# Layer 2's recurrence: half of the state scalings and most of the corner-block copies move from VectorE to ScalarE

## The chip, the cores and the metric

The program runs on one NeuronCore of a Trainium2 chip, in one launch. The metric is the device time in microseconds (us). The core's engines are named in the profile's short forms: PE (TensorE, matmuls), PEld (its weight loads), DVE (VectorE), ACT (ScalarE), POOL (GpSimd) and SP (SyncE, which issues most DMAs). Each engine runs its own instructions in program order and waits for the others on semaphores.

## The reference, cut to what matters

The model is one step of a decoder of four layers with a different token mixer in each. The prompt has 16 learned rows and 256 tokens, and eight sample sequences of 8 tokens ride along, so that 336 rows are carried through every layer. Layer 2 is RWKV-7 time mixing: 32 heads of 64 by 64 state, with a decay, and a rank-one correction of the state, at each token.

```
    def step(s, inp):
        r_t, w_t, k_t, v_t, a_t, b_t = inp
        sa = jnp.einsum('bhvk,bhk->bhv', s, a_t)
        s = s * w_t[:, :, None, :] + sa[..., None] * b_t[:, :, None, :] + v_t[..., None] * k_t[:, :, None, :]
        return s, jnp.einsum('bhvk,bhk->bhv', s, r_t)

    s_new, y = lax.scan(step, s0.astype(F32), (tm(r), tm(decay), tm(k), tm(v), tm(-kk), tm(kk * a)))
    ...
    out = (yn + bonus).reshape(b, l, D_INNER).astype(xn.dtype) * g
    return (xn[:, -1].astype(x_prev.dtype), s_new.astype(s0.dtype)), out @ p['w_o']
```

## The kernel before, in words

`layer2` replaces the token-by-token loop by chunks. The 336 rows make six units of 64 rows (`NU` is 6; unit 0 holds the samples, units 1 to 5 the prompt). The 32 heads are worked in 16 pairs (`KE` is 16; index `p`), one head on partitions 0 to 63 and one on 64 to 127, which is why most operations of this stage come twice, each on 64 partitions. A chunk needs the inverse of a unit triangular matrix. Its two 32 by 32 diagonal blocks are inverted row by row on DVE (`invert`: the products `tmpi` and the sums into `LT`), for all pairs in four lanes; the last lane still runs during the first six pairs of the recurrence.

Four functions, written as generators, make up the stage that the change touches:

- `before(p)` prepares a pair. It projects the values (`pvv`, 24 matmuls), builds the off-diagonal corner of the inverses in two products on PE (`pAZ`), and copies the result of each out of PSUM, two copies of 32 by 192 each: into `A_` (the second product's operand) and then into the right half of the tile `s.Z` (`Zr` in the profile). Then come the samples' start states (`pX`, copied to `x`) and the values transposed (`pvt`, copied into `SV` by DVE).
- `recur(p)` goes through the six units one after the other. In a unit: a product into `pch` and its copy `xs` (ACT); from unit 2 on the scaling `sd` of the carried state by the chunk's decay, one instruction of 64 by 64 per head; the product of the inverse with `xs`, and its copy into `SV` (ACT), over the rows that `sd` has read; then the state product, and one DVE instruction per head that multiplies it by the decay and adds `sd` (written `SV`, or `wo` in the last unit), and the output product into `pY`.
- `after(p)` normalises a finished pair: `ch` and `cl` are the two halves of `pY`, then `pm`, `sq`, `rln` (1 / the standard deviation, on ACT), `y`, and the gate's product on POOL.
- `sample(p)` updates the samples' states (`sx`, `S` on POOL and DVE, `pD` on PE).

Pair `p` takes two rounds of 18 slots; in each round the second half of one pair (units 3, 4, 5) runs beside the first half of the next (units 0, 1, 2). So unit 5 of `p` and unit 2 of `p + 1` are side by side, and their four scalings follow each other. The order inside a round is fixed by the table `PLAN` ("before", "after", "weights", "sample", "lanes" give the slots), and the four compute engines keep exactly this order (`InOrder`). In the rounds a weight block is split into high and low halves as well: `whi` on ACT, `wlo` on POOL.

The PSUM tile `pch` of a pair also holds the input of `rln`, so the next state product of the other half of that tile stands behind the read by `rln`. The start product of the next-but-one pair writes `pY` and stands behind the copy `cl<-pY` on DVE.

Of the kernel before, what the change touches and what calls it, by code (L numbers as in the profile page):

```python
# [12 lines left out]
AF = mybir.ActivationFunctionType  # L13
# [9 lines left out]
NS = 8  # L23
# [28 lines left out]
HB = 32  # L52
# [182 lines left out]
MUL, ADD, SUB = ALU.mult, ALU.add, ALU.subtract  # L235
# [193 lines left out]
def blocks(t):  # L429
    return [t[:, j] for j in range(t.shape[1])]  # L430
# [11 lines left out]
def dense_steps(k, out, parts, xh, xl, k0=0, n=8):  # L442

    hi, lo = parts
    for j in range(n):
        kk = k0 + j
        first, last = kk == 0, kk == len(xh) - 1
        k.nc.tensor.matmul(out, lo[:, j, :], xh[kk], start=first, stop=False)  # L448
        k.nc.tensor.matmul(out, hi[:, j, :], xl[kk], start=False, stop=False)  # L449
        k.nc.tensor.matmul(out, hi[:, j, :], xh[kk], start=False, stop=last)  # L450
        yield
# [902 lines left out]
def layer2(k, O):  # L1354
    nc, tc, A = k.nc, k.tc, k.A
# [10 lines left out]
    WC = keep.tile([P, KE, NS + NU - 1], F32, name="WC")  # L1366
# [296 lines left out]
    for n in range(2 * KE + 2):  # L1663
        p, t0 = n // 2, 8 * n
# [103 lines left out]
    top, low = ([slice(hp * HD + o, hp * HD + o + HB) for hp in range(2)] for o in (0, HB))  # L1768

    def before(p, x=None):  # L1770

        s = st[p]
        if p:
            pvv = k.ps.tile([P, 512], F32, tag="mm", name="pvv")[:, :N]
            x = dense_steps(k, pvv, W[p], blocks(vh), blocks(vl))
        else:
            x = iter(())
        ab = Ab[p % 2]
        for hp in range(2):
            nc.gpsimd.tensor_copy(ab[ss[hp], :, hp], s.A0[ss[hp]].rearrange("p w (b t) -> p b w t", t=TS))  # L1780
        for _ in range(3):
            next(x, None)
            yield

        pAZ = k.ps.tile([P, 512], F32, tag="az", name="pAZ")
        n = NU * HB
        A_ = tw.tile([P, NU, HB], F32, tag="A_", name="A_", bufs=1)
        for u in range(NU):
            for hp in range(2):
                nc.tensor.matmul(pAZ[low[hp], u * HB : (u + 1) * HB], s.L[top[hp], u], s.Z[top[hp], u, HB:], start=True, stop=True)  # L1790
        yield
        for hp in range(2):
            nc.vector.tensor_copy(A_[low[hp]].rearrange("p u c -> p (u c)"), pAZ[low[hp], :n])
        yield
        for _ in range(2):
            next(x, None)
            yield
        for u in range(NU):
            for hp in range(2):
                nc.tensor.matmul(pAZ[top[hp], n + u * HB : n + (u + 1) * HB], A_[low[hp], u], s.Z[low[hp], u, HB:], start=True, stop=True)  # L1800
        yield
        for hp in range(2):
            nc.vector.tensor_copy(s.Z[top[hp], :, HB:], pAZ[top[hp], n : 2 * n].rearrange("p (u c) -> p u c", c=HB))
        yield
        next(x, None)
        yield
        pX0 = k.ps.tile([P, 512], F32, tag="az", name="pX0")[:HD, : NS * 4 * TS]
        s.x0 = tw.tile([P, 2, NS, TS], F32, tag="x0", name="x0")
        for half in range(2):
            for b in range(half * NS // 2, (half + 1) * NS // 2):  # L1810
                nc.tensor.matmul(pX0[:, b * 4 * TS : (b + 1) * 4 * TS], s.S0[:, b], ab[:, b].rearrange("p g w t -> p (g w t)"), start=True, stop=True)
            if half == 0:
                for _ in range(2):
                    yield
                    next(x, None)
                if p:
                    nc.vector.tensor_copy(s.v[:, :N], pvv)
            yield
        pvt = k.ps.tile([P, 512], F32, tag="mm", name="pvt")[:, :NB]
        for j in range(3):  # L1820
            nc.tensor.transpose(pvt[:, j * P : (j + 1) * P], s.v[:, j * P : (j + 1) * P], k.ident)
        for hp in range(2):
            nc.scalar.copy(s.x0[vs[hp]].rearrange("p w b t -> p b w t"), pX0.rearrange("p (b g w t) -> p b g w t", g=2, w=2, t=TS)[:, :, hp])
        yield
        for j in range(2):
            for hp in range(2):
                nc.vector.tensor_copy(s.sv[vs[hp], j::2, hp], pvt[ss[j]].rearrange("p (u g c) -> p u g c", g=2, c=HD)[:, :, hp])
            yield
# [3 lines left out]
    def recur(p):  # L1832

        s = st[p]
        sv, G = s.sv, s.G
        s.c = k.ps.tile([P, 512], F32, tag=f"c{p % 2}", name="pch")
        pX, pA, pS = (s.c[:, j * HD : (j + 1) * HD] for j in (0, 0, 1))
        for u in range(NU):
            for hp in range(2):
                rows = slice(0, P) if u > 1 else vs[hp]  # L1840
                nc.tensor.matmul(pX[ss[hp]], G[rows, 0, hp, u], sv[rows, u, hp], start=True, stop=u > 0)
                if u == 0:
                    nc.tensor.matmul(pX[ss[hp]], s.x0[vs[hp], 1].rearrange("p b t -> p (b t)"), k.ident[vs[hp], vs[hp]], start=False, stop=True)
            xs = tw.tile([P, HD], F32, tag="xs", name="xs", bufs=2)
            nc.scalar.copy(xs, pX)
            yield
            if u == 0:
                s.Y = k.ps.tile([P, 512], F32, tag="Y", name="pY")[:, :NB]
            py = [s.Y[h, u * CH : (u + 1) * CH] for h in ss]
            if u > 1:  # L1850
                sd = tw.tile([P, HD], F32, tag="sd", name="sd", bufs=2)
                for hp, h in enumerate(ss):
                    nc.vector.tensor_scalar(sd[h], sv[h, u, hp], WC[h, p, NS + u - 1 : NS + u], None, op0=MUL)
            yield
            for hp in range(2):
                nc.tensor.matmul(pA[ss[hp]], s.Z[ss[hp], u], xs[ss[hp]], start=True, stop=True)
            yield
            for hp, h in enumerate(ss):
                if u > 1:
                    nc.tensor.matmul(py[hp], sv[h, u, hp], s.R[h, u], start=True, stop=False)  # L1860
                if u == 0:
                    nc.tensor.matmul(py[hp], k.ident[vs[hp], vs[hp]], s.x0[vs[hp], 0].rearrange("p b t -> p (b t)"), start=True, stop=False)
            for hp, h in enumerate(ss):
                nc.scalar.copy(sv[h, u, hp], pA[h])
            yield
            if u > 0:
                for hp in range(2):
                    nc.tensor.matmul(pS[ss[hp]], G[:, 2, hp, u], sv[:, u, hp], start=True, stop=True)
                if u < NU - 1:
                    o = [sv[h, u + 1, hp] for hp, h in enumerate(ss)]  # L1870
                else:
                    wo = tw.tile([P, HD], F32, tag="wo", name="wo", bufs=1)
                    o = [wo[h] for h in ss]
                for h, q in zip(ss, o):
                    d = WC[h, p, NS + u - 1 : NS + u]
                    if u == 1:
                        nc.vector.tensor_scalar(q, pS[h], d, None, op0=MUL)
                    else:
                        nc.vector.scalar_tensor_tensor(q, pS[h], d, sd[h], op0=MUL, op1=ADD)
            yield  # L1880
            for hp in range(2):
                nc.tensor.matmul(py[hp], sv[:, u, hp], G[:, 1, hp, u], start=u == 1, stop=True)
            if u == NU - 1:
                nc.sync.dma_start(O["wkv_p"][:, p], wo)
            yield
# [93 lines left out]
    def evacuate(i, out):  # L1979
        if items[i][0] is A["l2_v"]:  # L1980
            nc.scalar.copy(st[items[i][1]].v[:, :N], out)
            steps_.append(before(items[i][1]))
        else:
            gated(out)
# [49 lines left out]
    for t in range((KE + 1) * NT):  # L2034
        i, p = t % NT, t // NT - 1
# [30 lines left out]
        if i + 1 == NT and p + 3 < KE:  # L2066
            plan(before(p + 3), t, PLAN["before"])
# [333 lines left out]
```

## Time and profile before

| | |
|---|---|
| time before, median of 3 runs | 1878.07 us (1877.92 to 1886.85) |
| the profiled execution's own time | 1878.39 us |
| its span | 1876.5 us |
| mean granted TensorE clock | 0.953 of full speed |
| PE busy | 1738.5 us (93%) |
| DVE busy | 1213.3 us (65%) |
| ACT busy | 743.1 us (40%) |
| POOL busy | 641.4 us (34%) |
| first and last scaling `sd` | 1113.4 us and 1398.9 us |

Times inside the span count from the span's start. The rounds of the recurrence stand between about 1103 and 1402 us, some 300 us of the 1876.5. Line 382 is a helper that records almost every instruction of this stage, so instructions are told apart by their tiles. A row of the timeline gives the start, the time from the first to the last of the merged instructions, the engine, the operation, and in brackets how long the engine stood idle before and what ended that.

### The profile page before, as it was taken

The page shows a single profiled execution, that of the slowest core. Times are in us where ns is not written, and L with a number is a line of the kernel's source. Part 1 is how long each engine was busy: PE and PEld are TensorE (multiplying, and loading weights), DVE is VectorE, ACT ScalarE, POOL GpSimd, SP SyncE. Part 2 cuts the span into 40 slices and gives each one's busy share as a digit, 9 for nine tenths or more (in the row PEclk, how much of TensorE's full clock was granted, in tenths as well). Part 3 has the DMA queues.
Part 4 walks back from the last instruction along what each step waited for, and adds up shares of the span by engine and source line. Part 5 has one row for each costly group of instructions (what it writes and reads, how often), then busy time and mean ns, then how long its engine had stood idle before and what let it go on. Part 6 is the DMA issues. An engine that isn't in the chain of part 4 may idle for free. (4 is left out here: it accounts for less than half of the span.)

```text
span 1876.5 us, 32699 instructions
## 1 busy us (share of the span) xinstructions
PE 1738.5 (93%) x12302; PEld 1366.1 (73%) x12302; DVE 1213.3 (65%) x2304; ACT 743.1 (40%) x1738; POOL 641.4 (34%) x825
## 2 busy tenths in 40 slices
PE   4998897999999997999999998899989799999997
PEld 2666596867779996666666886677769578778776
DVE  8999547596435455655787858677765736355453
ACT  2553243432145343443445343355554324143332
POOL 5667334000000025434345343344446414142212
PEclk9999898999999998999998998789999899999998
DMA  5564544554564443356556864466623457666551
GB/s 194 136 169 130 129 150 142 162 170 132 152 169 151 142 147 99 115 173 194 176 180 190 246 199 133 126 192 187 183 90 102 149 179 242 216 198 240 180 192 68
DMA packets 199695, 306.16 MB, mean 163 GB/s; under 512 B 115601, under 2 KB 133777, under 8 KB 197041
## 3 DMA queue, kind: packets, MB, share of 16 engines
q1 hardware_dynamic: 178384, 265.84, 47.5%
q0 software_dynamic: 10592, 32.72, 5.3%
q10 hardware_dynamic: 10560, 5.51, 1.0%
q8 instruction: 97, 1.59, 0.4%
q14 instruction: 62, 0.50, 0.1%
HBM read 225.04 MB, written 78.97 MB: 162 GB/s over the span
## 5 line engine op out<-in xcount | busy, mean ns | idle before, releaser
L411 DVE TENSOR_TENSOR wlo<-wst,whi 128x1024 fp32r<-128x1024 f32 x138 | 171.2, 1242 | 158.1 <-ACT whi L407 132.2
L407 ACT CAST whi<-wst 128x1024 fp32r<-128x1024 f32 (+1 forms) x125 | 129.3, 1035 | 92.4 <-PE pr L450 39.1
L382 PE MATMUL pg<-x_n,wst 128*128 128x336 f32 x512 | 160.8, 458 | 0.0
L382 POOL TENSOR_TENSOR wlo<-wst,whi 128x512 fp32r<-128x512 f32 (+1 forms) x57 | 74.2, 1302 | 145.3 <-ACT whi L382 142.8
L382 PEld LDWEIGHTS pg<-x_n,wst 128*128 128x128 f32 x512 | 93.5, 191 | 41.4 <-issue 0.9
L382 PE MATMUL pu<-x_n,wst 128*128 128x336 f32 x352 | 114.8, 467 | 2.3 <-DVE x_n L491 1.8
L382 PE MATMUL pkr<-xr,wst 128*128 128x336 f32 x256 | 99.5, 485 | 0.0
L382 PEld LDWEIGHTS pu<-x_n,wst 128*128 128x128 f32 x352 | 67.7, 199 | 35.8 <-issue 3.2
L382 PEld LDWEIGHTS pgm<-AR,BK 64*128 64x128 f32 x384 | 58.2, 190 | 45.3 <-issue 25.2
L2311 DVE SCALAR_TENSOR_TENSOR s<-s,pn 128x512 f32<-128x512 f32 x64 | 43.8, 684 | 70.2 <-PE pn L2310 70.0
L569 POOL TENSOR_TENSOR sums<-sums 128x336 f32<-128x336 f32 x19 | 22.6, 1202 | 194.6 <-ACT sums L567 191.1
L382 ACT CAST whi<-wst 128x256 fp32r<-128x256 f32 (+1 forms) x117 | 68.0, 586 | 50.4 <-issue 14.1
L382 DVE TENSOR_TENSOR G<-pgm,gmask 128x128 f32<-128x128 f32 x192 | 46.3, 284 | 56.0 <-PE pgm L382 55.8
L382 PE MATMUL pgm<-AR,BK 64*128 64x128 f32 x384 | 80.2, 316 | 1.3 <-ACT G L382 1.3
L382 PE MATMUL pkr<-xk,wst 128*128 128x336 f32 x256 | 75.9, 446 | 0.0
L382 PEld LDWEIGHTS pch<-SV,Gr 128*64 128x64 f32 (+1 forms) x704 | 33.8, 145 | 56.6 <-ACT rln L382 20.0
L2312 POOL DMA_DIRECT2D out_ret_s<-s x32 | 17.2, 539 | 147.1 <-DVE s L2311 147.1
L450 PE MATMUL pz<-gh,whi 128*128 128x336 f32 x208 | 66.0, 317 | 0.0
L382 PEld LDWEIGHTS pkr<-xk,wst 128*128 128x128 f32 x256 | 48.7, 190 | 23.6
L448 PE MATMUL pz<-gh,wlo 128*128 128x336 f32 x208 | 65.9, 317 | 0.0
L449 PE MATMUL pz<-gl,whi 128*128 128x336 f32 x208 | 65.9, 317 | 0.0
L382 PE MATMUL pch<-SV,Gr 128*64 128x64 f32 (+1 forms) x704 | 51.0, 252 | 14.6 <-ACT rln L382 7.5
(807 smaller groups left out, 5374.6 us busy)
## 6 DMA issues: line engine op xcount, KB each, us to landing
wst<-in_l_in SPq DMA_DIRECT2D x64, 512.0 KB, 4.0
dG<-G SPq DMA_DIRECT2D x16, 1152.0 KB, 5.2
wst<-in_l_out SPq DMA_DIRECT2D x32, 512.0 KB, 3.8
wst<-in_l_glu SPq DMA_DIRECT2D x32, 512.0 KB, 3.8
wst<-in_l_g SPq DMA_DIRECT2D x32, 512.0 KB, 4.6
wst<-in_l_v SPq DMA_DIRECT2D x32, 512.0 KB, 4.6
s<-in_l_s SPq DMA_DIRECT2D x32, 512.0 KB, 4.1
out_ret_s<-s POOLq DMA_DIRECT2D x32, 512.0 KB, 4.8
```

What stands on the lines that cost most here:

```text
L382: return lambda *a, **kw: tc.keep_in_program_order(getattr(e, name)(*a, **kw))
L407: k.nc.scalar.copy(hf, st)
L411: e.tensor_tensor(lf[:, a:b], st[:, a:b], hf[:, a:b].bitcast(F32), op=ALU.subtract)
L448: k.nc.tensor.matmul(out, lo[:, j, :], xh[kk], start=first, stop=False)
L449: k.nc.tensor.matmul(out, hi[:, j, :], xl[kk], start=False, stop=False)
L450: k.nc.tensor.matmul(out, hi[:, j, :], xh[kk], start=False, stop=last)
L569: (nc.vector if m == KD - 1 and name != "xx" else nc.gpsimd).tensor_tensor(sums[name], sums[name], t, op=ADD)
L2311: nc.vector.scalar_tensor_tensor(s[:, d], s[:, d], math.exp(TS * LOG_G[h]), pn, op0=MUL, op1=ADD)
L2312: nc.gpsimd.dma_start(O["ret_s"][h, b], s)
```

## The change

In `before(p)` a name `copy` is ScalarE's copy for the first eight pairs and VectorE's for the others; the two copies into `A_` and the two into `Zr` go by it. In `recur(p)` the scalings `sd` of the even pairs become ScalarE activations with the function Copy and the decay as a scale operand per partition; those of the odd pairs stay on VectorE. No PE, POOL or DMA instruction changes its place, and no activation table is loaded that wasn't before.

```
+        copy = nc.scalar.copy if p < 8 else nc.vector.tensor_copy
...
-            nc.vector.tensor_copy(A_[low[hp]].rearrange("p u c -> p (u c)"), pAZ[low[hp], :n])
+            copy(A_[low[hp]].rearrange("p u c -> p (u c)"), pAZ[low[hp], :n])
...
-            nc.vector.tensor_copy(s.Z[top[hp], :, HB:], pAZ[top[hp], n : 2 * n].rearrange("p (u c) -> p u c", c=HB))
+            copy(s.Z[top[hp], :, HB:], pAZ[top[hp], n : 2 * n].rearrange("p (u c) -> p u c", c=HB))
...
-                    nc.vector.tensor_scalar(sd[h], sv[h, u, hp], WC[h, p, NS + u - 1 : NS + u], None, op0=MUL)
+                    d = WC[h, p, NS + u - 1 : NS + u]
+                    if p % 2:
+                        nc.vector.tensor_scalar(sd[h], sv[h, u, hp], d, None, op0=MUL)
+                    else:
+                        nc.scalar.activation(sd[h], sv[h, u, hp], AF.Copy, scale=d)
```

On DVE, early in the round in which pair 0 does units 3 to 5: two scalings and two copies stand between the inversion's steps (`tmpi`, `LT`).

```order
 L382 TENSOR_TENSOR tmpi<-LT 128x135
 L382 TENSOR_TENSOR LT<-LT,tmpi 128x27x5
-L382 TENSOR_SCALAR sd<-SV_8904,WC 64x64 x2
-L382 COPY A__9850<-pAZ 32x192 x2
 L382 TENSOR_TENSOR tmpi<-LT 128x156
 L382 TENSOR_TENSOR LT<-LT,tmpi 128x26x6
```

Both leave DVE there; the inversion's steps close up.

On DVE, at the end of the next round, where unit 5 of pair 1 (`SV_8905`) and unit 2 of pair 2 (`SV_8906`) are side by side, ahead of the copies of the transposed values and the last state of pair 1:

```order
 L382 TENSOR_TENSOR LT<-LT,tmpi 128x18x14
 L382 TENSOR_SCALAR sd<-SV_8905,WC 64x64 x2
-L382 TENSOR_SCALAR sd<-SV_8906,WC 64x64 x2
 L382 COPY SV_8904<-pvt 64x3x64 x4
 L382 SCALAR_TENSOR_TENSOR wo<-pch,WC,sd 64x64 x2
```

Two of the four scalings leave DVE; the odd pair's two stay.

On ACT, the same place, in the kernel before:

```order
L382 COPY xs<-pch 128x64 x2
L382 COPY x_10201<-pX_10200 64x8x2x8 x2
L382 CAST whi<-wst 128x256
L382 COPY SV_8905<-pch 64x64 x2
L382 COPY SV_8906<-pch 64x64 x2
L382 ACTIVATE rln<-pch,b_10257 128x336
```

and in the changed kernel:

```order
L382 COPY xs<-pch 128x64 x2
L382 ACTIVATE sd<-SV_8906,WC 64x64 x2
L382 COPY x_10201<-pX_10200 64x8x2x8 x2
L382 CAST whi<-wst 128x256
L382 COPY SV_8905<-pch 64x64 x2
L382 COPY SV_8906<-pch 64x64 x2
L382 ACTIVATE rln<-pch,b_10257 128x336
```

The two scalings of the even pair stand between `xs` and the copies into `SV`, one after the other, and `rln` follows.

## Rows read from the trace of the kernel before

**Rows 1.** Busy time by stretch: length, PE, PEld, DVE, ACT, POOL, clock, DMA.

```profile
1115.00:1133.00 18.00, 15.30 (x225) 11.77 (x225) 15.91 (x42) 6.33 (x26) 6.23 (x7) 1.00 0.35 90
1280.00:1300.00 20.00, 19.30 (x292) 14.88 (x291) 14.93 (x43) 11.36 (x40) 9.26 (x10) 1.00 0.70 201
```

**Rows 2.** DVE's timeline: the last states of pairs 0, 1, 5 and 6.

```profile
1132.47 0.60 DVE L382 SCALAR_TENSOR_TENSOR wo<-pch,WC,sd 64x64 f32<-64x64 f32 x2
...
1150.65 0.60 DVE L382 SCALAR_TENSOR_TENSOR wo<-pch,WC,sd 64x64 f32<-64x64 f32 x2
...
1241.36 0.60 DVE L382 SCALAR_TENSOR_TENSOR wo<-pch,WC,sd 64x64 f32<-64x64 f32 x2 [0.93 <-ACT rln L382]
...
1257.29 0.60 DVE L382 SCALAR_TENSOR_TENSOR wo<-pch,WC,sd 64x64 f32<-64x64 f32 x2 [0.93 <-ACT rln L382]
```

**Rows 3.** PE's timeline, 1115 to 1225 us: matmuls before which PE stood idle.

```profile
1115.32 0.34 PE L382 MATMUL pch<-SV,Gr 128*64 128x64 f32 x4 [0.41 <-ACT SV L382]
...
1119.78 0.34 PE L382 MATMUL pch<-SV,Gr 128*64 128x64 f32 x4 [0.46 <-ACT SV L382]
...
1122.29 0.60 PE L382 MATMUL pch<-SV,Gr 128*64 128x64 f32 x8 [1.06 <-DVE SV L382]
...
1131.40 0.34 PE L382 MATMUL pch<-SV,Gr 128*64 128x64 f32 x4 [0.68 <-ACT SV L382]
...
1133.75 0.60 PE L382 MATMUL pch<-SV,Gr 128*64 128x64 f32 x8 [0.66 <-DVE SV L382]
...
1139.78 0.60 PE L382 MATMUL pch<-SV,Gr 128*64 128x64 f32 x8 [0.70 <-DVE SV L382]
...
1150.15 0.45 PE L382 MATMUL pch<-SV,Gr 128*64 128x64 f32 x8 [1.56 <-ACT rln L382]
...
1155.99 0.33 PE L382 MATMUL pY<-x,ident 64*64 64x64 f32 x4 [2.18 <-DVE cl L382]
...
1172.77 0.45 PE L382 MATMUL pch<-SV,Gr 128*64 128x64 f32 x8 [1.00 <-ACT rln L382]
...
1196.30 0.45 PE L382 MATMUL pch<-SV,Gr 128*64 128x64 f32 x8 [0.74 <-ACT rln L382]
...
1219.41 0.45 PE L382 MATMUL pch<-SV,Gr 128*64 128x64 f32 x8 [0.37 <-ACT rln L382]
...
1224.80 0.33 PE L382 MATMUL pY<-x,ident 64*64 64x64 f32 x4 [1.79 <-DVE cl L382]
```

**Rows 4.** The scalings: all of them (ns min/median/max), then one place in the timeline.

```profile
L382 DVE TENSOR_SCALAR sd<-SV,WC x128: 233/253/1354, 1113.4 to 1398.9; 64x64 f32<-64x64 f32 x128
...
1147.07 2.18 DVE L382 TENSOR_SCALAR sd<-SV,WC 64x64 f32<-64x64 f32 x4
1147.08 1.27 POOL L382 TENSOR_TENSOR wlo<-wst,whi 128x512 fp32r<-128x512 f32 x1 [3.74 <-ACT whi L382]
...
1148.49 1.06 ACT L382 COPY SV<-pch 64x64 f32<-64x64 f32 x4 [1.48 <-DVE sd L382]
```

**Rows 5.** Groups by shape, 1103 to 1402 us: busy us, mean ns, idle before.

```profile
L382 ACT COPY xs<-pch 128x64 f32<-128x64 f32 x96 | 19.4, 212 | 81.3 <-PE pch L382 74.7 <-DVE tmpi L382 3.6 <-DVE SV L382 2.3
L382 ACT ACTIVATE rln<-pch,b 128x336 f32<-128x336 f32 x15 | 8.1, 540 | 0.2
L382 ACT COPY x<-pX 64x128 f32<-64x128 f32 x30 | 7.7, 258 | 2.8 <-PE pX L382 2.6
...
L382 DVE COPY Zr<-pAZ 32x192 f32<-32x192 f32 x30 | 10.5, 350 | 18.2 <-PE pAZ L382 17.9
```

**Rows 6.** ACT's timeline between `xs` and `SV`, where pair 4 does its unit 5.

```profile
1216.62 0.53 ACT L382 COPY x<-pX 64x128 f32<-64x128 f32 x2 [0.18 <-PE pX L382]
...
1217.95 0.86 ACT L382 COPY SV<-pch 64x64 f32<-64x64 f32 x4 [0.49 <-PE pY L382]
```

**Rows 7.** Two stretches around a fall of the clock, columns as in rows 1.

```profile
1222.20:1225.60 3.40, 1.61 (x44) 1.16 (x42) 2.93 (x7) 0.97 (x4) 2.42 (x4) 1.00 0.52 151
1225.60:1229.00 3.40, 3.40 (x28) 2.31 (x25) 3.13 (x9) 2.53 (x4) 1.04 (x1) 0.59 0.64 178
```

## The prediction

> **What bounds the kernel now.** The change touches only layer 2's rounds, so I read that stage alone. First the busy time by stretch [rows 1]. From 1280 to 1300 us, a stretch without the inversion, PE is busy 19.30 of 20 us: PE bounds it. From 1115 to 1133, with the inversion's steps on DVE, PE is busy 15.30 of 18 and DVE 15.91: there DVE sets the pace. ACT has 6.33 of 18 us in use and 11.36 of 20.
>
> Then the distance between the last states of successive pairs gives the time of a round [rows 2]: 1150.65 - 1132.47 = 18.18 us for pair 1's, (1241.36 - 1150.65) / 4 = 22.68 for those of pairs 2 to 5, and 1257.29 - 1241.36 = 15.93 for pair 6's. Against the last, which is PE's own pace, the rounds with the inversion lose 2 to 7 us each.
>
> Where these go, PE's own waits tell [rows 3]. The reader is to see three kinds. In the rounds of pairs 0 and 1, PE waits for copies into SV by ACT or for states by DVE. At a pair's end it waits for `rln`: 1.56, 1.00, 0.74, 0.37 us. And a little later it waits 2.18 and 1.79 for `cl` (the same wait, about 2 us, stands in the rounds of pairs 3 and 4 too). The last kind also moves the clock [rows 7]: in the 3.4 us to 1225.6 PE is busy 1.61 us at the full clock, and in the next 3.4 the granted clock averages 0.59, since it falls to its lower level (1.2 GHz). This happens once in each of the rounds of pairs 2 to 5 and makes 18.18 into 22.68, so one such fall costs about 4.5 us.
>
> **What the scalings do there** [rows 4]. Most of the 128 take 253 ns, the longest 1354. At 1147.07 four of them take 2.18 us, the first beside a POOL product that runs from 1147.08 to 1148.35. ACT's copies into SV overwrite what the scalings read; ACT has been idle 1.48 us for them, `rln` follows those copies, and PE's 1.56 us is the end of this chain. So a scaling can cost PE more than its own time.
>
> **Removed from DVE.** 64 scalings and 32 copies of 350 ns [rows 5]. What that is worth is read off PE's waits, one by one [rows 3].
>
> At 1115.32 and 1119.78 PE waits 0.41 and 0.46 us for copies behind scalings of pair 0, which move: both go, 0.87. At 1122.29 it waits 1.06 for states of DVE, behind a pair of scalings and a pair of `A_` copies: 2 x 0.253 + 2 x 0.350 = 1.21, more than the wait, so all of 1.06 goes; next late is PE itself. At 1131.40 (0.68) four scalings stand ahead, two stay: I take 0.40. At 1133.75 (0.66) the state stands behind the same four: 2 x 0.253 = 0.51, I take 0.50. At 1139.78 (0.70) two `A_` copies, 0.70, stood ahead: all of it. Sum 3.5 us. Bounds: 2.3 (only the three waits for DVE's states, 1.06 + 0.50 + 0.70) and 4.0 (all six whole).
>
> The waits for `rln` have a floor, the 0.37 of 1219.41, where no scaling was held up. Down to it there is 1.19 + 0.63 + 0.37 = 2.2 us. Two of four scalings stay on DVE at each place. I take all 2.2, since DVE has some 1.2 us less to do ahead of them in a round and should reach them before POOL's product starts. The lower bound, if they are held up as now, is the two moved ones' own time in the first place only, 0.5.
>
> By the Trainium skill (SBUF — State Buffer, section "SBUF: two separate sides") a VectorE instruction in a two-port mode and a GpSimd one exclude each other for the whole instruction, which fits the scaling beside the POOL product. By that rule alone the two that stay remain exposed, this term is its lower bound 0.5, and the sum below would end 1.7 us later.
>
> In the rounds of pairs 2 to 5 the rest gains nothing: after `cl` PE has no wait of weight until the clock is back. From pair 6's round on, PE is the bound, with nothing to win there.
>
> **Added to ACT.** The trace has no 64-wide activation with an operand per partition. Below it lies the copy `xs`, 64 wide, 212 ns; above it `rln`, with such an operand but 336 wide, 540 ns [rows 5]. Width costs (258 - 212) / 64 = 0.72 ns a column, so 540 - 272 x 0.72 = 344 ns, which I take, being the same form; a pair is 0.69 us, between 0.42 and 1.08.
>
> At the end of a pair two of them stand between `xs` and the copies into SV, in every round. Room there, where DVE holds nothing up, is ACT's own idle: 0.18 + 0.49 = 0.67 us [rows 6]. What is queued behind is `rln`, and PE behind that without slack. So SV comes 0.02 us late; for the wait between two dependent activations I allow 0.1. From pair 5's round to pair 14's that is 10 x 0.1 = 1.0 us lost (earlier rounds have it inside the terms above). Bounds: 0, and at 1.08 us a pair 0.41 x 10 = 4.1. At units 3 and 4 the same pair costs nothing: PE has the corner products, `pvv` and `pY` between its product with `xs` and the next that reads SV.
>
> By the Trainium skill (ScalarE: Activation LUTs, section "What ACT_TABLE_LOAD costs") an activation takes 186 ns + 0.833 ns a column and 93 more per pointer operand. An estimate from that page is 332 ns each and, with its overlap of 93, 0.57 us a pair: inside the room, so this term would be 0 and the end 1.0 us earlier.
>
> The `A_` and `Zr` copies come to 212 + 128 x 0.72 = 304 ns, a pair 0.61 us. They stand behind SV copies and ahead of `whi` and the next `xs`; ACT is idle 81.3 / 96 = 0.85 us before an `xs` on average, which covers 0.61. Bare of that cover each pair would cost up to 0.6. Those of pairs 0 and 1 come before the recurrence, where they end no wait of PE. DVE stood waiting for PE before them 17.9 us in all; ACT inherits the wait, but reaches that place later than DVE did, after SV.
>
> **The sum.** -3.5 - 2.2 + 1.0 = -4.7 us. The profiled execution took 1878.39 us, which becomes 1873.7. The median of the runs is 0.3 lower, so 1873.4. With the clock as before, the bounds give -4.0 - 2.2 + 0 = -6.2 (1871.9) and -2.3 - 0.5 + 1.0 = -1.8 (1876.3).
>
> **Why the clock stays as it is.** The wait for `cl` is a chain on DVE from the last state over SV, two `y`, `S` and one step of the inversion to `cl`. No scaling and no corner copy stands in it. At 1224.80 the wait was 1.79 us with the `rln` wait already at its floor, and the clock fell all the same [rows 3, 7].
>
> **Rivals.**
>
> (a) A fall of the clock goes away, because the idle ahead of it shrinks (1.56 to 0.37 at 1150) or lies otherwise. Each is worth 4.5 us: 1868.9 for one, 1864.4 for two. For it: the round of pair 1 has waits of 0.66 and 0.70 and no fall, so there is a limit between. Against it: the four falls each stand behind an untouched wait of about 2 us. 0.22 in all: one 0.12, more 0.10.
>
> (b) Slower than before: ACT becomes late at each pair's end. At the upper price of 1.08 a pair, SV and `rln` come 0.41 us later in 15 rounds, 6.2 us; the waits for SV copies and `rln` then stay, and only 1.06 + 0.50 + 0.70 = 2.3 is won: 1878.1 + 3.9 = 1882.0. It decides from 0.67 + 2.3 / 15 = 0.82 us a pair. For it: the room of 0.67 is nearly used up at my price. Against it: the wide `rln` is a poor model of a 64-wide scaling. 0.08. The Trainium skill (ScalarE: Activation LUTs, section "Rules for kernel authors") points this way: it gives multiplications to VectorE, not ScalarE. Here the row of 253 ns against the 344 worked out agrees in the bare price; what speaks for ACT is the hold-up to 1354 ns.
>
> (c) The waits are hidden elsewhere: what pairs 0 and 1 win is given back at the next wait for `cl`, and the scalings that stay are held up as now. Then only 0.87 + 0.5 - 1.0 = 0.4 us remains: 1877.7. 0.10.
>
> (d) One fall of the clock more, in a round that had none, since the falls depend on how waits lie: 1873.4 + 4.5 = 1877.9, two 1882.4. 0.06.
>
> **How the numbers follow.** The forecast, 1873.4 with 1871.9 to 1876.3, has 0.54. The range takes in one and two falls fewer at the lower end (1864) and one more, and most of (b), at the upper: 1864 to 1881. About 0.5% (9.4 us) is what a measurement of this kernel can tell from no change. Faster than 1868.7: two falls fewer 0.10, half of one fewer 0.06, and 0.06 for the forecast with larger terms, 0.22. Slower than 1887.5: the tails of (b) and (d), 0.07. No change 0.71.
>
> **What the changed profile would show.** Right: PE's waits of 0.41, 0.46, 1.06 and 0.70 us in the first two rounds are gone; those for `rln` stand near 0.4 in every round; rounds of pairs 0 and 1 near 16.5 us, of pair 6 on near 16.0; `sd` on ACT near 0.34 us; the `cl` wait still about 2 us and four falls of the clock. Wrong, if the half-clock stretches number other than four before 1240, if `sd` on ACT takes over 0.4 us with SV waiting behind it, or if the rounds from pair 6 on exceed 16.2 us.

## The result, and the profile after

The changed kernel takes 1870.74 us (median of 20 runs, 1858.28 to 1879.85), the kernel before 1884.41 us in the 20 runs beside it. The ratio is 0.9927 with a 95% interval of 0.9912 to 0.9942: 13.7 us less, where the sum gave 4.7. The time lies inside the range; but the three runs shown beforehand were on the low side (1878.07 against 1884.41), so the gain is three times the forecast, outside the sum's own bounds of 1.8 to 6.2 us, and two thirds of it have to be found somewhere else than in the sum. Moved by the same 6.3 us, the range of 1864 to 1881 would be 1870.3 to 1887.3, with the time at its very edge: that it was hit is partly luck.

The profiled execution took 1874.76 us with a span of 1872.8. First the kernel before by rounds, in the columns of [rows 1]: pair 0's with its start, pair 1's, those of pairs 2 to 5 together, and the rest.

```profile
1103.80:1132.47 28.67, 25.78 (x367) 19.55 (x366) 21.88 (x58) 11.67 (x42) 10.86 (x11) 1.00 0.39 105
1132.47:1150.65 18.18, 14.55 (x216) 10.67 (x214) 16.81 (x41) 7.54 (x28) 6.39 (x7) 1.00 0.58 167
1150.65:1241.36 90.71, 79.56 (x874) 60.52 (x870) 66.92 (x172) 38.09 (x123) 29.02 (x32) 0.74 0.48 142
1241.36:1401.01 159.65, 149.57 (x1999) 111.70 (x1993) 122.87 (x321) 84.23 (x297) 69.62 (x76) 0.98 0.54 160
```

The same four stretches of the changed kernel, cut at the same places (pair 0's first product into `pch`, then the last states of pairs 0, 1, 5 and 15):

```profile
1106.05:1131.93 25.88, 24.50 (x359) 18.95 (x360) 13.76 (x40) 15.90 (x57) 10.56 (x11) 1.00 0.37 106
1131.93:1148.81 16.88, 15.37 (x227) 11.50 (x225) 14.31 (x36) 9.78 (x35) 6.69 (x8) 1.00 0.61 182
1148.81:1235.77 86.96, 75.33 (x876) 56.91 (x872) 55.73 (x140) 47.50 (x156) 29.74 (x32) 0.78 0.49 150
1235.77:1394.59 158.82, 146.62 (x1999) 109.55 (x1993) 108.42 (x283) 95.13 (x335) 69.70 (x76) 0.99 0.53 161
```

The reader is to see two things. Where the clock stands at 1.00, the rounds of pairs 0 and 1 are 2.79 and 1.30 us shorter. In the rounds of pairs 2 to 5 the granted clock rose from 0.74 to 0.78. It has two levels, full and half (1.00 and 0.50 in stretches shown below), so twice what the mean lacks to 1 is the share of the time at the lower level: 2 x 0.26 x 90.71 = 47.2 us at the lower level became 2 x 0.22 x 86.96 = 38.3. The stage as a whole gave 297.2 - 288.5 = 8.7 us in these two profiles. The span fell by only 3.7, since the stretches outside the stage were 5.0 us longer in this execution.

PE's waits, which answer to [rows 3], from the round of pair 1 to that of pair 5:

```profile
1135.78 0.33 PE L382 MATMUL pY<-x,ident 64*64 64x64 f32 x4 [0.59 <-DVE cl L382]
1142.99 0.62 PE L382 MATMUL pX<-Ab,S 128*64 128x32 f32 x8 [0.55 <-issue]
1148.37 0.45 PE L382 MATMUL pch<-SV,Gr 128*64 128x64 f32 x8 [0.37 <-ACT rln L382]
1154.13 0.48 PE L382 MATMUL pY<-x,ident 64*64 64x64 f32 x4 [2.15 <-DVE cl L382]
...
1171.20 0.45 PE L382 MATMUL pch<-SV,Gr 128*64 128x64 f32 x8 [0.42 <-ACT rln L382]
1176.95 0.33 PE L382 MATMUL pY<-x,ident 64*64 64x64 f32 x4 [2.14 <-DVE cl L382]
1194.33 0.45 PE L382 MATMUL pch<-SV,Gr 128*64 128x64 f32 x8 [0.37 <-ACT rln L382]
1199.94 0.33 PE L382 MATMUL pY<-x,ident 64*64 64x64 f32 x4 [1.98 <-DVE cl L382]
1213.64 0.45 PE L382 MATMUL pch<-SV,Gr 128*64 128x64 f32 x8 [0.70 <-ACT rln L382]
1219.02 0.33 PE L382 MATMUL pY<-x,ident 64*64 64x64 f32 x4 [1.76 <-DVE cl L382]
1224.62 0.45 PE L382 MATMUL pch<-xs,Zr 64*64 64x64 f32 x8 [1.67 <-ACT xs L382]
```

All the waits for SV are gone and `rln` is at its floor save once, 0.70. The four waits for `cl` stand as before. New are 0.55 us marked "issue", which means that the profile shows nothing that PE waited for (two more such waits, 0.73 us at 1116.90 and 0.37 at 1126.98, stand in pair 0's round), and 1.67 us for `xs`, which stands behind the inversion's last copy (2.00 us) and an activation (1.15) on ACT.

There are four falls of the clock again, but the last one does not stand right behind its wait for `cl`. After that wait the clock is full for more than 5 us, and it falls behind the new wait for `xs`:

```profile
1218.60:1224.20 5.60, 3.94 (x56) 2.68 (x56) 3.14 (x11) 4.77 (x9) 1.43 (x3) 1.00 0.67 226
1224.60:1232.00 7.40, 7.38 (x82) 6.42 (x82) 3.07 (x7) 4.30 (x13) 2.72 (x2) 0.54 0.58 204
```

The scalings, answering to [rows 4] (ns, min/median/max):

```profile
L382 ACT ACTIVATE sd<-SV,WC x64: 342/346/351, 1115.1 to 1375.1; 64x64 f32<-64x64 f32 x64
L382 DVE TENSOR_SCALAR sd<-SV,WC x64: 233/254/1277, 1130.0 to 1392.5; 64x64 f32<-64x64 f32 x64
```

On ACT none is held up; on DVE the longest still takes 1277 ns.

### The profile page after: what moved, and what is told of

Its sections match the earlier page's. It is cut to its first block, busy times and chain, and to the rows that moved or that the text cites. A ratio compares the mean times of both kernels' runs of the same rounds, so it can differ in the third digit from the quotient of the medians.

```text
span 1872.8 us, 32683 instructions
## 1 busy us (share of the span) xinstructions
PE 1733.1 (93%) x12302; PEld 1360.0 (73%) x12302; DVE 1176.4 (63%) x2208; ACT 771.0 (41%) x1834; POOL 645.2 (34%) x825
## 4 chain that ended last, share of the span: by engine, by line
PE 60%; DVE 9%; ACT 4%; issue 3%; DMA 2%; POOL 2%; SPq 0%; ACTq 0%; DVEq 0%; POOLq 0%
PE pkr L382 8%; PE pg L382 6%; PE pgm L382 4%; PE pz L448 3%; PE pz L449 3%; PE pz L450 3%; PE pvv L382 3%; PE pch L382 3%; PE pu L382 3%; PE py L382 2%; PE py L2304 2%; PE pv L382 1%; DMA wst<-in_l_o 1%; PE pz L382 1%; PE pY L382 1%
## 5 line engine op out<-in xcount | busy, mean ns | idle before, releaser
L2304 PE MATMUL py<-s,qs 128*72 128x512 f32 x128 | 59.4, 591 | 0.0
```

Of the source, the lines that this page charges most:

```text
L2304: nc.tensor.matmul(read.py0, qs[:, d, b * NSAM : b * NSAM + QW], states[h * NS + b][:, d], start=b + d == 0, stop=b + d == NS)
```

## The experiments

My theory was the sum: hold-ups on DVE removed, the clock left as it was. The main rival was (a): the clock. A second was lateness on ACT, (b).

**The change in its two parts.** Scalings alone:

```
-        copy = nc.scalar.copy if p < 8 else nc.vector.tensor_copy
+        copy = nc.vector.tensor_copy
```

> Only the state scalings of even pairs go to ScalarE; the corner copies of all pairs stay on VectorE. If the gain is the removed hold-ups alone (the prediction's sum), this part has 0.87 + 0.40 + 0.50 us of the waits in the rounds of pairs 0 and 1 and the 2.2 us of the waits for rln, and loses nothing in steady rounds: 4.0 us, a ratio of 0.998 to the kernel before, half-clock stretches as before. If most of the gain comes from the clock (a stretch at 1.2 GHz shortened or gone), a part that leaves the waits for cl where they are may lie anywhere between 0.993 and 1.0, but its time then goes with its mean granted clock: about 0.5 us less for each us less at the lower level.

Copies alone:

```
-                    if p % 2:
+                    if True:
                         nc.vector.tensor_scalar(sd[h], sv[h, u, hp], d, None, op0=MUL)
```

> Only the corner copies of the first eight pairs go to ScalarE; all scalings stay on VectorE. By the hold-ups alone: the wait of 0.70 us at 1139.78 and 0.70 of the 1.06 us at 1122.29, so 1.4 us, a ratio of 0.999, and the waits for rln stay at 1.56, 1.00 and 0.74 us. If the copies were what shortens the half-clock stretches, this kernel has most of the gain, 0.994 to 0.996, with a mean granted clock of 0.956 to 0.960 as the changed kernel has.

The scalings alone give 1876.55 us, ratio 0.9946 (0.9922 to 0.9971); the copies alone 1882.41, 0.9976 (0.9957 to 0.9996). The two add up to the whole change, 0.54% + 0.24% = 0.78% against 0.73%, and the first is more than twice its hold-ups (10.2 us against 4.0). The second, 4.5 us against 1.4, has an interval of 0.8 to 8.1 us, which takes in the 1.4. The mean granted clock over the 12 runs of each was 0.955 and 0.956, against 0.951 in 29 runs of the kernel before. So the copies alone raised the clock as much as the scalings did and gained less than half as much: the mean clock of whole runs is a rough yardstick.

The profile of the scalings alone shows what a wait for `cl` can do and leave undone. A wait in PE's timeline, then by stretch the round of pair 4 in which it stands and the rounds of pairs 2 to 5 together:

```profile
1199.86 0.33 PE L382 MATMUL pY<-x,ident 64*64 64x64 f32 x4 [2.00 <-DVE cl L382]
```

```profile
1194.70:1212.66 17.96, 15.25 (x225) 11.29 (x221) 14.72 (x39) 10.23 (x37) 7.26 (x8) 1.00 0.58 167
...
1153.87:1234.29 80.42, 70.09 (x876) 52.75 (x872) 60.79 (x156) 42.78 (x140) 29.01 (x32) 0.85 0.54 162
```

The wait of 2.00 us is there, the clock does not fall, and the round takes 17.96 us where the same round of the changed kernel took 19.31 and that of the kernel before, with nearly the same waits (2.02 us for `cl` and 0.37 for `rln`, here 2.00 and 0.42), 23.04. So the prediction's reckoning of one fall of 4.5 us behind each wait of 2 us does not hold.

With the copies alone PE still waits 1.00 us for `rln` at 1147.71 and again at 1189.84: it is the scalings that bring these waits to their floor. The copies in turn bring the one wait for `rln` that grew: it is 0.71 us at 1211.80 in their run, 0.42 at the same place with the scalings alone.

**Both kernels again,** to see how much of this is chance:

> The kernel before, unchanged, for its clock in many executions and a second profile. By hold-ups alone its mean granted clock should be that of the changed kernel (0.953 to 0.964 over 20 executions) and its time 4.7 us longer at the same clock. If the clock carries the rest, its granted clock is lower by 0.003 to 0.004 in the mean (about 6 us more at the lower level), and the second profile again has some 48 us at the lower level in the rounds of pairs 2 to 5, against 37 in the changed kernel.

> The changed kernel once more, for a second profile beside the kernels of this study. Ratio 0.9927 again. If the clock carries two thirds of the gain, its half-clock stretches in the rounds differ from those of the first profile (13.65, 13.65, 3.41, 6.83 us) though the waits for cl are the same four, and the total lies below the 47.8 us that both profiles of the kernel before show; the time of the rounds follows it by about 0.5 us for each us. If the hold-ups alone made the gain, the second profile shows stretches near 47.8 us too and the same gain.

The kernel before gave 1.0004 (0.9984 to 1.0025), the changed one 1873.82 us, 0.9935 (0.9910 to 0.9959). The rounds of pairs 2 to 5 by stretch, the kernel before:

```profile
1159.09:1249.53 90.44, 79.61 (x873) 60.53 (x870) 66.89 (x171) 38.03 (x123) 29.01 (x32) 0.74 0.47 141
```

and the changed kernel:

```profile
1153.08:1235.27 82.19, 71.89 (x876) 53.73 (x872) 56.33 (x139) 47.67 (x156) 29.63 (x32) 0.83 0.53 158
```

The kernel before repeats itself: 0.74 and 47.0 us at the lower level, as in the first profile. The changed kernel does not: 0.83, 27.9 us, where it had 38.3. Its two profiles differ by 86.96 - 82.19 = 4.77 us for 10.4 us at the lower level. That gives the price of the clock within one kernel, 0.46 us for each us. By it the clock explains 8.9 x 0.46 = 4.1 of the 3.75 us between the first profiles of the two kernels, and 19.1 x 0.46 = 8.8 of the 8.3 between the second ones. In these four rounds the gain is the clock's.

Over all executions: a mean granted clock of 0.958 in 20 runs of the changed kernel, against 0.951, 0.952 and 0.953 in the three sets of the kernel before (29, 24 and 11 runs, each set on another chip). At 0.952 that is 2 x 0.006 x 1880 = 23 us less at the lower level, and 23 x 0.46 = 10 of the 13.7 us. On one and the same chip, in the second set of the changed kernel's runs, it is 0.9577 against 0.9532, 2 x 0.0045 x 1880 = 17 us, so 8 of 12.7. The rest, 4 to 5 us, is near the 4.1 us that the rounds of pairs 0 and 1 gave at the full clock. The split is an estimate. A straight line through the 20 runs of the changed kernel has a price of 0.48, one through the 29 of the kernel before 0.35; one thousandth of the clock is 1.7 us; and of the 2 x 0.047 x 1876.5 = 176 us at the lower level in the first profile only 47 lie in these four rounds.

**What the falls follow.** The inversion step between `S` and `cl` is moved to another place of the round:

```
-    "lanes": (3, 5, 9, 11, 17),
+    "lanes": (3, 5, 9, 9, 11),
```

> The changed kernel with the fifth inversion step of a round moved from between S and cl on VectorE (slot 17) to the one at slot 9, where VectorE then idles 2.4 to 2.7 us. The wait for cl of about 2 us in the rounds of pairs 2 to 5 should fall to the 0.3 us of later rounds. If these waits are what the falls of the clock follow, the falls go too and the four rounds (22.83 + 23.13 + 19.31 + 21.69 us) go to 15.9 each: 23 us less than the changed kernel, near 1847 us, 0.981 of the kernel before. If only the waits go and the clock falls as before: 4 x 1.7 = 6.8 us less, near 1864 us, 0.989. If another wait takes their place: no change from 0.993.

1860.04 us, 0.9867 (0.9836 to 0.9897): between the two numbers, and nearer to that of the waits alone. In PE's timeline every wait for `cl` is near 0.3 us, and two others have come up:

```profile
1170.68 0.33 PE L382 MATMUL pY<-x,ident 64*64 64x64 f32 x4 [0.31 <-DVE cl L382]
1178.05 0.79 PE L382 MATMUL pch<-SV,Gr 128*64 128x64 f32 x8 [1.18 <-ACT SV L382]
...
1214.92 0.45 PE L382 MATMUL pch<-xs,Zr 64*64 64x64 f32 x8 [2.18 <-ACT xs L382]
```

The first is late by two scalings that stayed on DVE, beside a POOL product (POOL's and DVE's timelines):

```profile
1176.17 1.19 POOL L382 TENSOR_TENSOR sx<-bmask,SV 128x512 f32<-128x512 f32 x1
...
1176.38 1.31 DVE L382 TENSOR_SCALAR sd<-SV,WC 64x64 f32<-64x64 f32 x2
```

By stretch, right ahead of the fall, behind it, and pairs 2 to 5 together:

```profile
1176.60:1180.00 3.40, 1.56 (x22) 1.04 (x21) 3.19 (x9) 2.30 (x8) 0.76 (x1) 0.90 0.77 201
1180.00:1188.00 8.00, 8.00 (x54) 5.96 (x54) 3.82 (x12) 3.85 (x14) 1.26 (x1) 0.50 0.17 34
...
1150.13:1224.68 74.55, 67.14 (x876) 50.46 (x872) 57.54 (x137) 47.59 (x156) 29.79 (x32) 0.91 0.58 175
```

So the falls moved with the waits: two are left of four. The round of pair 4, where the longest wait is 0.70 us, took 16.2 us; one fall stands behind 1.18 us of waiting for SV and 0.55 marked "issue", the other behind the 2.18 for `xs`.

The same move in the kernel before:

> The kernel before, with nothing of the change, but with the inversion step moved from between S and cl (slot 17) to slot 9, as in the changed kernel's run of the same edit (0.9867). The waits for cl of 2.2 to 1.8 us should fall to 0.3, as there. If the change's worth is its hold-ups alone, this kernel lies 5 to 6 us above that run: 0.990. If most of the change's worth was that half-clock stretches, set off by the waits for cl, ended sooner, little of it is left once these waits are gone, and this kernel comes within 3 us of that run, 0.987 to 0.988. If the hold-ups that the change removes set off falls by themselves, this kernel keeps some: waits for SV and rln of 0.7 to 1.5 us followed by a fall, and 0.993 or more.

1878.51 us, 0.9956 (0.9939 to 0.9973): the third case. PE's timeline has waits for DVE that the change removes, two of them

```profile
1168.47 0.60 PE L382 MATMUL pch<-SV,Gr 128*64 128x64 f32 x8 [1.31 <-DVE SV L382]
...
1191.03 0.70 PE L382 MATMUL pch<-SV,Gr 128*64 128x64 f32 x8 [1.26 <-DVE SV L382]
```

and a fall stands behind each of the two (by stretch; the last row has pairs 2 to 5):

```profile
1170.50:1178.00 7.50, 6.82 (x63) 5.78 (x58) 6.94 (x17) 2.58 (x9) 1.71 (x2) 0.53 0.24 65
1191.00:1198.50 7.50, 7.47 (x79) 6.33 (x80) 7.14 (x16) 2.88 (x10) 2.46 (x2) 0.54 0.51 160
...
1160.62:1244.02 83.40, 72.56 (x873) 54.67 (x870) 71.61 (x170) 38.17 (x123) 28.48 (x32) 0.84 0.51 153
```

On top of the moved step the change is worth 0.9956 - 0.9867 = 0.89%, some 17 us. The two intervals leave 0.5 to 1.2%, so this can't be told from the 0.73% that it is worth by itself.

**The waiting kept, PE given work.** Ahead of the product that waits for `cl`, matmuls whose result nobody reads:

```
+            if u == 0 and 3 <= p <= 6:
+                for _ in range(24):
+                    nc.tensor.matmul(s.c[:, 464:512], k.ident, k.ident[:, :48], start=True, stop=True)
```

> The changed kernel with 24 matmuls that compute nothing of use (128x48, into free columns of pch) ahead of the pY product that waits for cl, in the rounds of pairs 2 to 5. VectorE still hands over cl as late as before, so the waiting itself stays, but TensorE works through it. If the falls of the clock follow TensorE's idling there, the half-clock stretches in these rounds go (37.5 us in the changed kernel's profile) and the rounds fall to about 17.8 us each: 15 us less, near 0.985. If the falls come from elsewhere, no gain: 0.993, or above it by what the 24 matmuls overrun the wait.

1891.33 us, 1.0019 (1.0002 to 1.0036). This was a poor test: one row of PE's timeline shows the filler taking 5.88 us, nearly three times the wait it should fill (the profile has 48 records for the 24 matmuls).

```profile
1155.70 5.88 PE L382 MATMUL pch<-ident 128*128 128x48 f32 x48
```

By stretch it shows something else, though: PE is busy throughout, as the profile counts it with modelled ends of the matmuls, and the clock falls all the same.

```profile
1157.00:1159.00 2.00, 2.00 (x21) 2.00 (x19) 1.64 (x4) 0.00 (x0) 0.88 (x3) 1.00 0.67 191
1159.00:1161.00 2.00, 2.00 (x20) 2.00 (x19) 0.00 (x0) 0.00 (x0) 0.00 (x0) 0.94 0.82 260
1161.00:1163.00 2.00, 2.00 (x32) 1.73 (x32) 0.00 (x0) 0.60 (x3) 1.03 (x1) 0.50 0.29 120
```

Twelve wide ones instead, `nc.tensor.matmul(s.c[:, 2 * HD : 2 * HD + N], less, blocks(vh)[0], start=True, stop=True)`:

> The run with 24 matmuls of 128x48 ahead of the pY product was no test of the wait alone: they took 5.88 us, three times the wait, and the clock fell with TensorE busy throughout. Here 12 matmuls of 128x336 that compute nothing of use stand there, at 0.155 us each as the pvv products beside them: 1.9 us, inside the wait of 2.1. If the falls follow TensorE's lack of work in the wait for cl, the half-clock stretches of the rounds of pairs 2 to 5 go and these rounds take 17.5 to 18 us each, 15 us less than the changed kernel, near 0.985. If the falls come from elsewhere, nothing is gained: 0.993 or, where the 12 run at the lower clock, 0.994 to 0.996.

1866.85 us, 0.9897 (0.9874 to 0.9921), between the two numbers, with four times 2.1 us of useless work. PE's timeline and the rounds of pairs 2 and of 2 to 5 by stretch:

```profile
1156.22 2.13 PE L382 MATMUL pch<-xvh,less 128*128 128x336 f32 x12
1158.45 0.33 PE L382 MATMUL pY<-x,ident 64*64 64x64 f32 x4
```

```profile
1153.12:1170.89 17.77, 17.18 (x237) 13.18 (x233) 15.50 (x35) 11.42 (x41) 7.65 (x8) 1.00 0.57 169
...
1153.12:1231.28 78.16, 73.22 (x924) 56.00 (x920) 56.80 (x140) 47.66 (x156) 29.98 (x32) 0.93 0.55 167
```

Pair 2's round takes the 17.5 to 18 us forecast for it: `cl` still comes when it did, the clock stays at 1.00. So it does in the rounds of pairs 4 and 5 (18.07 and 19.38 us, the second with 1.46 us of waiting for `xs`). Only one of the four falls is left, in the round of pair 3 (clock 0.78), behind another wait (0.99 us for SV at 1183.05). `cl` is as late as ever here, so it is what PE does in the wait, and not the late `cl` itself, that the clock follows in these rounds. Over all runs it is 0.964 in the mean here and 0.958 in the changed kernel's runs on the same chip. With the narrow filler PE was busy too, as the profile counts it, and the clock fell.

**ScalarE's room.** All scalings on ACT:

```
-                    if p % 2:
+                    if False:
```

> The changed kernel with the scalings of all pairs on ScalarE. At a pair's end four scalings of 0.346 us then stand between xs and the copies into SV: 1.38 us against a room of 0.67. By the prediction's own reckoning of ScalarE's lateness (its rival b) every round from pair 6 on is 0.5 to 0.7 us longer than the changed kernel's 15.66 and 15.91, with rln late: +5 to +7 us, a ratio of 0.996 to 0.997. If ScalarE has more room than that, since the even rounds were already 0.25 us shorter than the odd ones, all rounds go to 15.66 and the rest of the hold-ups on VectorE go too: 0.990 to 0.992.

1879.45 us, 0.9968 (0.9951 to 0.9986): rival (b)'s mechanism. At a pair's end (ACT's timeline, then PE's) four scalings stand behind `xs`, and PE waits longer for `rln` than its 0.37:

```profile
1297.45 1.46 ACT L382 ACTIVATE sd<-SV,WC 64x64 f32<-64x64 f32 x4
```

```profile
1301.12 0.45 PE L382 MATMUL pch<-SV,Gr 128*64 128x64 f32 x8 [0.62 <-ACT rln L382]
```

Its later rounds take 1317.77 - 1301.56 = 16.2 us, where the changed kernel's take 15.66 (1314.58 - 1298.92) and 15.91 (1330.49 - 1314.58). With two scalings ACT has room, with four it has not.

**The waits taken away together.** Step at slot 7 instead of 17, scalings of pairs up to 6 on ACT, the last inversion's copy in quarters and the activation behind it in halves (and its later steps spread over one round more):

```
-    "lanes": (3, 5, 9, 11, 17),
+    "lanes": (3, 5, 7, 9, 11),
...
-                    if p % 2:
+                    if p % 2 and p > 6:
...
-        nc.scalar.copy(L, T.rearrange("p r c -> p c r"))
+            nc.scalar.copy(L[:, g], T[:, :, g].rearrange("p r c -> p c r"))
+            if n == 2:
+                yield
```

> The changed kernel with the inversion step at slot 7 in place of 17, the scalings of all pairs up to 6 on ScalarE (the odd ones beside POOL took 1.31 us and were followed by a wait of 1.18 and a fall in the run with the step moved), and the last inversion's copy LT in four pieces of a quarter each, in place of the copy of 2.0 us and the activation of 1.15 that held up xs for 1.67 us. No wait of PE above 0.8 us should stay in the rounds of pairs 1 to 6. If falls follow such waits, none is left in these rounds, each takes 15.7 to 16.2 us, and the time is near 1846 us, 0.980. If the clock falls for another reason: 0.986 to 0.988.

1857.07 us, 0.9856 (0.9829 to 0.9882). By stretch, pairs 2 to 5:

```profile
1152.27:1220.56 68.29, 61.42 (x876) 45.51 (x872) 52.54 (x121) 50.30 (x173) 29.68 (x32) 1.00 0.60 175
```

No fall is left in these rounds, which take 18.7 us less than in the changed kernel's first profile and 13.9 less than in its second. The rounds take 16.4 to 17.6 us, not 16, as `rln` is late by the four scalings (0.62) and states by the two steps of the inversion side by side. The time did not come to 0.980: against the changed kernel's 0.9927 it is 0.71%, some 13 us. By the time alone the second number, 0.986, would fit as well; that the falls are gone is read from the clock of 1.00 above.

Then with the steps and the scalings placed once more:

```
-    "lanes": (3, 5, 7, 9, 11),
+    "lanes": (3, 5, 7, 11, 12),
...
-                    if p % 2 and p > 6:
+                    if p % 2 and (p > 6 or u + 1 == NU):
```

> As the kernel with the waits removed (0.9856, rounds of pairs 2 to 6 of 16.4 to 17.6 us and none at the lower clock), but the step at slot 9 goes to slot 12, behind the states of units 2 and 5 that waited 0.54 and 0.28 us for VectorE, and at a pair's end the odd pairs' scalings stay on VectorE, since four on ScalarE made the wait for rln 0.62 in place of 0.37 to 0.42. If these are what is left in the rounds, each of pairs 2 to 6 loses 0.5 to 1.2 us: 0.983. If VectorE's scalings at the pair's end are held up by POOL again, the wait for rln goes to 0.7 or more and falls return: 0.987 or above.

1859.29 us, 0.9865 (0.9835 to 0.9894): no further gain. Its rounds of pairs 2 to 5 take 67.24 us in all, 1.05 less, but PE now waits 2.26 us for `xs` at 1227.82, and that round, pair 6's, takes 18.87 us where it took 16.82. Two waits for DVE's states have come up in the other rounds, 1.03 us at 1147.20 and one in the row below, and no fall follows them (PE's timeline; pairs 2 to 5 by stretch):

```profile
1181.12 0.60 PE L382 MATMUL pch<-SV,Gr 128*64 128x64 f32 x8 [1.14 <-DVE SV L382]
```

```profile
1145.96:1213.20 67.24, 60.08 (x862) 44.52 (x862) 52.71 (x124) 48.72 (x167) 29.87 (x32) 1.00 0.59 177
```

The three versions with the step moved, 0.9856 to 0.9867, can't be told apart; all beat both kernels.

## Why the prediction was right in part

**The hold-ups: right in kind, about right in sum.** They are best counted on PE's own products. From pair 0's first product to the one that had waited 0.66 us it takes 1133.75 - 1103.83 = 29.92 us before and 1133.31 - 1106.05 = 27.26 after: 2.66 less, where the terms were 0.87 + 1.06 + 0.40 + 0.50 = 2.83. From there to the product that waits for `rln` it takes 1150.15 - 1133.75 = 16.40 us before and 1148.37 - 1133.31 = 15.06 after: 1.34 less, where the terms were 0.70 + 1.19 = 1.89, and the new 0.55 us marked "issue" is what is missing. That the first part comes so close is partly luck, since the new waits of 0.73 and 0.37 us stand in it, which no term had.

**The waits for `rln`: right save one.** 0.37, 0.42, 0.37 and 0.70 us against the 0.37 that was taken as floor: 1.19 + 0.58 + 0.37 - 0.33 = 1.8 us for the 2.2 of the sum, and not the lower bound of 0.5 by the two scalings that stay. The rule of the Trainium skill (SBUF — State Buffer, section "SBUF: two separate sides"), that a VectorE and a GpSimd instruction can lock each other out for the whole instruction, agrees with the 1.31 us of two scalings beside POOL's 1.19 in the run with the step moved, and with the scalings on ACT, which never took more than 351 ns. In the changed kernel two such scalings at a pair's end took 0.53 us at 1191.68 and at 1210.57, free of POOL's product.

**ScalarE's lateness: a term too large, beside a gain that the sum didn't have.** +1.0 us was expected in all; the rounds from pair 6 on are 0.83 us shorter in sum. The scaling itself was sized right (346 ns, expected 344), and so was the pair (0.71 us, expected 0.69), but what follows it does not wait for its end. In ACT's timeline of the changed kernel

```profile
1295.16 0.35 ACT L382 COPY xs<-pch 128x64 f32<-128x64 f32 x2 [1.62 <-PE pch L382]
1295.41 0.71 ACT L382 ACTIVATE sd<-SV,WC 64x64 f32<-64x64 f32 x2
1296.03 0.51 ACT L382 COPY x<-pX 64x128 f32<-64x128 f32 x2
```

the next instruction starts 0.62 us after the first scaling, below the room of 0.67. The Trainium skill (ScalarE: Activation LUTs, section "What ACT_TABLE_LOAD costs") has successive activations overlap by some 93 ns. The trace agrees for the copy, which starts 0.09 us before the scalings end, and not for the two scalings, of which the second starts 0.37 us after the first. That page's estimate of 0.57 us a pair is therefore too short, though it set the term rightly to about 0. What lateness there is shows as 0.43 us for `rln` in place of 0.37 at the end of every second round.

The gain beside it is read from the rounds of pairs 6 to 12, which run at the full clock in both kernels (before, then after):

```profile
1241.36:1352.86 111.50, 106.63 (x1527) 80.11 (x1523) 87.80 (x238) 59.32 (x211) 48.97 (x56) 1.00 0.64 185
1235.77:1346.18 110.41, 105.38 (x1527) 79.31 (x1523) 77.22 (x208) 67.74 (x241) 49.04 (x56) 1.00 0.62 187
```

They are 1.09 us shorter with the same count of matmuls, by some 0.25 us in each even pair's round. It comes with the scalings: their run alone has rounds of 15.66 and 15.91 us too, that of the copies alone 15.92 to 15.94. In an even round PE is busy some 0.3 us less; why is open.

**The clock: the step that failed.** "Why the clock stays as it is" reasoned that no scaling stands in the chain to `cl`, so the waits of 2 us stay and their falls with them. The waits did stay. What failed is the step from them to the clock, one fall of 4.5 us behind each, and with it the sum's leaving the clock at nothing, where an estimated 8 to 10 us came. The same wait is followed by a short stretch at the lower level, a long one or none, and over many executions the changed kernel has some 17 to 23 us less of it. This was rival (a) with 0.22, thought of as falls that go away; the four falls are still there in both profiles of the changed kernel, only shorter in sum. Falls of the clock also follow waits that the change does remove, as the run with the step moved in the kernel before shows. The limit of length that (a) saw between waits of 0.70 and 2 us doesn't show: 1.18 us with 0.55 behind it were followed by a fall, waits of 1.03, 1.14 and 2.00 us were not.

**Its signs.** The waits (save the 0.70), the price of a scaling and the four falls came as named. Pair 1's round takes 16.88 us, not 16.5. Of the rounds from pair 6 on, which were not to exceed 16.2 us, pair 13's and pair 15's do (16.27 and 16.28). And the range, said to take in most of (b), ends at 1881, below (b)'s own 1882.0.

**What stays open.** Why the falls became shorter is argued only as far as the runs with the waits filled or taken away go. Which of the removed waits shortened which stretch isn't settled. Single profiles of one kernel differ (38.3 and 27.9 us), and the two parts of the change alone have 24.1 (2 x 0.15 x 80.42) and 34.7 us (2 x 0.20 x 86.87) in one profile each, the first less than the whole change has in either of its two.

## What to carry to other kernels

Where TensorE waits a microsecond or two in a stage and the granted clock falls behind it, a wait costs its own length and can cost some 5 us more (17.96 against 23.04 us for one round here). A sum of waits leaves that out, so the clock needs a term of its own with a chance of its own. Look for the instruction that can simply stand elsewhere on the late engine: one inversion step moved from ahead of `cl` was worth another 0.6%. And an engine that gets work has room for so much: two scalings were free, four cost 0.3 to 0.5 us a round.

## What was not expected of the hardware

TensorE's clock fell to its lower level while the profile, which models where a matmul ends, showed it busy 2.00 of 2 us, in a row of matmuls of 48 columns, in the kernel with the narrow filler. Useless matmuls in a wait made the kernel faster: 1866.85 us against 1873.82 for the same kernel without them on the same chip.
